# Mixture-of-experts stage of a hybrid layer: GpSimd's arithmetic goes to VectorE, and each tile's weights are written in 16 transfers

## The chip, the cores and the metric

The kernel runs on one core of one Trainium2 chip. The metric is the time of one execution on the device, in microseconds (us). The core has a matrix engine (TensorE, PE in the profile), three engines for elementwise work (VectorE or DVE, ScalarE or ACT, GpSimd or POOL), SyncE (SP), which here only issues transfers, and 16 DMA engines that carry the transfers of all queues.

## The reference

One layer over 512 latent and 256 context tokens of width 1024: a scan (mLSTM) and grouped-query attention side by side, a norm, and then a PEER stage, a product-key mixture of 16384 experts with one hidden unit each. The change lies in the PEER stage and in the norm behind it:

```python
def block(xt):                                   # 128 tokens
    q = (xt @ wq).reshape(P_BLOCK, P_HEADS, 2, P_HALF)
    s = jnp.einsum('nhpd,hpkd->nhpk', q, keys)
    s1, i1 = lax.top_k(s[:, :, 0], P_TOPK)       # 16 of 128 keys, twice for each of 8 heads
    s2, i2 = lax.top_k(s[:, :, 1], P_TOPK)
    cand_s = (s1[..., :, None] + s2[..., None, :])...
    cand_i = (i1[..., :, None] * N_KEYS + i2[..., None, :])...
    top_s, pos = lax.top_k(cand_s, P_TOPK)       # 16 of the 256 pairs
    idx = jnp.take_along_axis(cand_i, pos, axis=-1).reshape(P_BLOCK, P_HEADS * P_TOPK)
    g = jax.nn.softmax(top_s)...
    act = jax.nn.gelu(jnp.einsum('nd,ned->ne', xt, u[idx]), approximate=False)
    return jnp.einsum('ne,ned->nd', g * act, v[idx])
...
x = _layer_norm(DEEPNORM_ALPHA * x + g2 * y, ln2_g[l], ln2_b[l])
```

## The kernel before

Up to about 430 us run the modulation, the projection, the scan, the attention, the output projection and the first norm. The change does not touch them.

From 430 to 570 us comes the head of the PEER stage. `scores` multiplies the tokens with the query weights (line 838) and the queries with the keys (line 846), for two tiles of 128 tokens at a time. `select(t)` finds the top 16 on VectorE. Its part `weigh` turns the position of each chosen pair into two key indices: the position is split into its two ranks (lines 933 to 942), and each rank picks its index by a one-hot comparison with 0 to 15 (line 952, VectorE, f32), a multiply with the 16 indices (line 954, GpSimd) and a reduction over 16 (line 962, VectorE). A cast on GpSimd (line 930) makes the indices f32 first. `prelude(t)` then builds, from one-hot matrices A and B and matmuls (lines 1008 to 1023), the dense table of weights, 128 tokens by 16384 experts, in the tile `work`: 64 KB of each partition. Four transfers of 2 MB on SP's queue write it to the tensor `Wd[t]` in memory (line 1028), each partition's share of a transfer being one run of 16 KB. Then `tables` and `look_up` list the experts that any token of the tile chose.

From 617 to 1253 us run the blocks: four tiles of 29 blocks with 128 experts each. For each block GpSimd issues gathers (line 1108): 128 expert rows of 8 KB (`uv`, 1 MB) and the block's weights from `Wd[t]` (`wr`, 64 KB). A dense block (17 of a tile) transposes the expert rows (line 1268), multiplies them with the tokens (line 1282), applies Gelu on ScalarE (line 1283) and multiplies with the weights on VectorE (line 1284, tile `wt`). A gathered block (12 of a tile) holds experts that one token alone chose: VectorE finds the token (line 1147), GpSimd gathers its row from `h2d` (`xg`, 0.5 MB), VectorE takes the products (line 1168). Both end in two matmuls that add to the tile's result (line 1196, `py`).

Two step lists set the order around the change. In the head, `HEADS` says behind which steps of `select(0)` and `prelude(0)` a query step of tiles 2 and 3 is put. During the blocks of tile t, the generator `ahead` runs `select(t+1)` and `prelude(t+1)`; each step of it has a cost in the list `cost`, and behind each block as many steps are issued as keep the spent cost in line with the blocks done. A scheduler then fixes each engine's order from dependences and priorities. An engine works its instructions in that order, and so does each queue.

When a tile is through, `finish` does the second norm in steps between the next tile's blocks (lines 1248 to 1259): the residual is loaded on GpSimd's queue, the scale and the offset on ScalarE's; VectorE makes the sum (line 1251) and normalises (line 745), GpSimd multiplies with the scale (line 1255) and adds the offset (line 1258).

## Time and profile before

| | |
|---|---|
| median of three runs | 1260.15 us (1259.62 to 1260.58) |
| profiled execution | 1269.07 us |
| its span in the profile | 1267.3 us |
| TensorE (PE) busy | 1051.4 us, 83% |
| VectorE (DVE) busy | 850.2 us, 67% |
| ScalarE (ACT) busy | 467.2 us, 37% |
| GpSimd (POOL) busy | 523.0 us, 41% |
| DMA | 284.16 MB, mean 224 GB/s |
| last chain, by engine | PE 45%, DVE 13%, DMA 9%, issue 5% |

The durations below come from the one profiled execution; a sum made of them is set against its own 1269.07 us. The span runs from the first to the last instruction. The last chain follows the work that ended last back to its start and shares the span out among what it went through. An engine that is busy while another one holds the path costs nothing, and one that waits on the path costs time however little it does. Names such as `work` and `uv` are those of tiles; "xg<-h2d,ti" is an operation that writes `xg` and reads `h2d` and `ti`.

### The profile page before, as it was taken

The page shows a single profiled execution, that of the slowest core. Times are in us where ns is not written, and L with a number is a line of the kernel's source. Part 1 is how long each engine was busy: PE and PEld are TensorE (multiplying, and loading weights), DVE is VectorE, ACT ScalarE, POOL GpSimd, SP SyncE. Part 2 cuts the span into 40 slices and gives each one's busy share as a digit, 9 for nine tenths or more (in the row PEclk, how much of TensorE's full clock was granted, in tenths as well). Part 3 has the DMA queues.
Part 4 walks back from the last instruction along what each step waited for, and adds up shares of the span by engine and source line. Part 5 has one row for each costly group of instructions (what it writes and reads, how often), then busy time and mean ns, then how long its engine had stood idle before and what let it go on. Part 6 is the DMA issues. An engine that isn't in the chain of part 4 may idle for free.

```text
span 1267.3 us, 19149 instructions
## 1 busy us (share of the span) xinstructions
PE 1051.4 (83%) x6784; PEld 844.8 (67%) x6784; DVE 850.2 (67%) x2655; ACT 467.2 (37%) x1132; POOL 523.0 (41%) x404
## 2 busy tenths in 40 slices
PE   6899779699999999993678848769878599597885
PEld 5788679598888888993457725558546477364653
DVE  5958989588857776757748728978479686223123
ACT  4342343555550122444315424234443244432221
POOL 4642423321053411003475513666444755355660
PEclk7899889699999999996789978879988799798988
DMA  9656431310046796228666795488996588988893
GB/s 364 222 200 227 140 134 35 116 41 3 1 151 216 226 264 191 60 91 344 247 255 248 253 364 187 153 293 307 345 410 227 216 291 323 414 314 302 326 350 120
DMA packets 102127, 284.16 MB, mean 224 GB/s; under 512 B 8548, under 2 KB 61512, under 8 KB 83976
## 3 DMA queue, kind: packets, MB, share of 16 engines
q0 software_dynamic: 28480, 158.62, 34.2%
q1 hardware_dynamic: 67656, 115.59, 26.0%
q10 hardware_dynamic: 5888, 8.65, 2.0%
q8 instruction: 55, 0.90, 0.3%
q14 instruction: 48, 0.39, 0.1%
HBM read 237.17 MB, written 45.66 MB: 223 GB/s over the span
## 4 chain that ended last, share of the span: by engine, by line
PE 45%; DVE 13%; DMA 9%; issue 5%; ACT 2%; POOL 2%; another core or an unknown queue 1%; DVEq 0%; ACTq 0%; POOLq 0%
PE py L1196 11%; PE pwq L838 8%; PE s L1282 6%; PE pW L1021 5%; DMA xg<-h2d,ti 5%; PE put L1268 2%; PE pf L1018 2%; DMA wr<-Wd,wi 2%; PE pw L769 2%; PE po L541 2%; DVE work L900 1%; PE ppt L567 1%; DVE work L897 1%; DVE work L898 1%; PE psc L846 1%
## 5 line engine op out<-in xcount | busy, mean ns | idle before, releaser
L1196 PE MATMUL py<-uv,wt 128*128 128x512 f32 x464 | 247.5, 654 | 25.1 <-DVE wt L1284 10.8
L1108 POOL DMA_INDIRECT uv<-in_uv,ri x116 | 120.8, 1041 | 131.9 <-PE py L1196 72.9
L1282 PEld LDWEIGHTS s<-ht,ut 128*128 128x128 f32 x1088 | 143.3, 205 | 40.6 <-ACT wt L1283 21.5
L1282 PE MATMUL s<-ht,ut 128*128 128x128 f32 x1088 | 152.5, 292 | 18.9 <-ACT wt L1283 17.9
L1108 POOL DMA_INDIRECT wr<-Wd,wi x116 | 121.2, 1045 | 54.8 <-issue 29.1
L1196 PEld LDWEIGHTS py<-uv,wt 128*128 128x128 f32 x464 | 84.4, 206 | 83.2 <-issue 54.8
L1269 ACT COPY ut<-put 128x512 f32<-128x512 f32 x136 | 75.3, 588 | 132.1 <-PE put L1268 85.1
L1021 PEld LDWEIGHTS <-A 128*128 128x128 f16 x1024 | 92.7, 147 | 23.1 <-issue 17.4
L1023 ACT ACTIVATE work<-pW 128x512 f32<-128x512 f32 x128 | 74.3, 597 | 89.7 <-PE pW L1021 64.8
L1021 PE MATMUL pW<-B,A 128*128 128x128 f16 x1024 | 98.0, 229 | 9.7 <-ACT work L1023 5.9
L1108 POOL DMA_INDIRECT xg<-h2d,ti x48 | 58.9, 1228 | 96.7 <-DVE ti L1148 44.9
L1268 PE MATMUL put<-cst,uv 128*128 128x128 f32 x544 | 79.4, 286 | 23.2 <-DMA uv<-in_uv,ri 14.4
L1268 PEld LDWEIGHTS put<-cst,uv 128*128 128x128 f32 x544 | 65.8, 149 | 47.3 <-issue 29.4
L838 PE MATMUL pwq<-h2T,wq 128*128 128x256 f32 x416 | 95.0, 380 | 0.0
L1168 DVE SCALAR_TENSOR_TENSOR xg<-xg,uv 128x1024 f32<-128x1024 f32 x48 | 58.6, 1220 | 49.7 <-DMA xg<-h2d,ti 49.7
L1018 PE MATMUL pf<-B,A 128*128 128x128 f16 x512 | 81.3, 230 | 10.5 <-DVE B L1011 10.5
L1011 DVE TENSOR_TENSOR B<-B,igr 128x1024 f16<-128x1024 f16 x128 | 83.3, 687 | 1.2
L838 PEld LDWEIGHTS pwq<-h2T,wq 128*128 128x128 f32 x416 | 76.8, 190 | 9.4 <-DMA wq<-in_wq 0.2
L1018 PEld LDWEIGHTS <-A 128*128 128x128 f16 x512 | 64.2, 148 | 22.2 <-issue 14.5
L1008 DVE TENSOR_TENSOR A<-iob,ig 128x1024 f16<-128x1024 f16 x64 | 46.5, 727 | 48.3 <-PE pW L1021 28.0
L208 POOL TENSOR_TENSOR wlo<-wi,whi 128x1024 fp32r<-128x1024 f32 (+1 forms) x18 | 48.5, 2711 | 59.9 <-ACT whi L207 59.8
L1284 DVE TENSOR_TENSOR wt<-wt,wr 128x128 f32<-128x128 f32 x68 | 25.7, 378 | 63.4 <-ACT wt L1283 52.9
(437 smaller groups left out, 2382.5 us busy)
## 6 DMA issues: line engine op xcount, KB each, us to landing
Wd<-work SPq DMA_DIRECT2D x16, 2048.0 KB, 22.1
wm<-in_w_modT SPq DMA_DIRECT2D x16, 1024.0 KB, 5.0
wq<-in_wq SPq DMA_DIRECT2D x26, 512.0 KB, 4.9
wi<-in_w_in SPq DMA_DIRECT2D x8, 1024.0 KB, 5.5
wsc<-in_w_mod SPq DMA_DIRECT2D x7, 1024.0 KB, 15.6
wor<-in_w_out SPq DMA_DIRECT2D x8, 512.0 KB, 4.2
wql<-in_wq SPq DMA_DIRECT2D x6, 512.0 KB, 5.6
qkT<-in_w_in SPq DMA_DIRECT2D x2, 1024.0 KB
```

Of the source, the lines that this page charges most:

```text
L208: nc.gpsimd.tensor_tensor(lo[:, k:k + 4, 0:cw], wv[:, k:k + 4], hi[:, k:k + 4, 0:cw].bitcast(F32), op=ALU.subtract)
L838: nc.tensor.matmul(pt, w[:, k, :], h2T[:, k, t0 * P:(t0 + 2) * P], start=k == 0, stop=k == KC - 1)
L1011: nc.vector.tensor_tensor(B[:, q].rearrange("p a n r -> p a (n r)"), (B[:, 0] if q else ior).rearrange("p a n r -> p a (n r)"), igr[:, q, ...
L1018: nc.tensor.matmul(pf[:, 0:P], A[:, :, n], B[:, 0, :, n, :], start=c == 0 and n == 0, stop=c == P // TCH - 1 and n == TCH - 1)
L1021: nc.tensor.matmul(pw[:, (n - n4) * P:(n - n4 + 1) * P], A[:, :, n], B[:, q, :, n, :], start=q == 1, stop=q == 2)
L1023: nc.scalar.mul(Wn[:, :, n0 + n4:n0 + n4 + 4], pw.rearrange("p (n k) -> p k n", n=4), 1.0 / GSC)
L1108: nc.gpsimd.indirect_dma_start(out=dst, out_offset=None, in_=src, in_offset=bass.IndirectOffsetOnAxis(ap=ids, axis=0))
L1168: nc.vector.scalar_tensor_tensor(xg, xg, 1.0, w[:, 0:D], op0=ALU.mult, op1=ALU.mult, accum_out=nf)
L1196: nc.tensor.matmul(py[:, hs], wt, w[:, D + half * 512:D + half * 512 + 512], start=i == 0, stop=i == n - 1)
L1268: nc.tensor.transpose(pt[:, q * P:(q + 1) * P], w[:, (4 * kh + q) * P:(4 * kh + q + 1) * P], ident)
L1269: nc.scalar.copy(ut[:, 4 * kh:4 * kh + 4, :], pt.rearrange("p (q n) -> p q n", q=4))
L1282: nc.tensor.matmul(s_[:, 0:P], ut[:, k, :], ht[:, k, :], start=k == 0, stop=k == KC - 1)
```

## The change

GpSimd loses all its arithmetic in the PEER stage. The cast of the indices goes to VectorE and makes f16 (`sih`). The one-hot comparison is made in f16 for all eight heads of a half at once (2048 elements of each partition; 1024 in tile 0, which works on four heads at a time) against a constant `place`, with the sixteen positions in the last dimension but one; the multiply is on VectorE, and four halving adds take the place of the reduction. The norm's two GpSimd instructions become two VectorE instructions that include the normalisation, so that line 745 is no longer called there; its three loads all go to SP's queue, and two more `yield`s stand between its steps. The table of weights goes out in 16 transfers of 512 KB (4 KB of each partition) in place of four; the function `send` issues one behind each later step of `ahead`, and what is left when the first block of the tile comes; in tile 0 all go at once. The costs and `HEADS` change with it.

```diff
-C_SEL, C_OH, C_IIG, C_A, C_L, C_N = 5, 1.5, 6, 3.5, 1.5, 1
+C_SEL, C_OH, C_IIG, C_A, C_L, C_N = 5, 3, 2, 3.5, 1.5, 1
+WPC = 16
...
-HEADS = tuple(range(3, 35, 2))
+HEADS = (2, 4, 6, 8, 10, 12, 14, 16, 18, 21, 24, 27, 30, 33, 38, 40)
...
-            nc.gpsimd.tensor_copy(sif[:, hs].rearrange("p h q a -> p (h q) a"), si[:, 2 * h0:2 * (h0 + gh)])
+            nc.vector.tensor_copy(sih[:, hs].rearrange("p h q a -> p (h q) a"), si[:, 2 * h0:2 * (h0 + gh)])
...
-            n4 = min(gh, 4)
             for q in range(2):
-                for g0 in range(0, gh, n4):
...
-                    nc.vector.tensor_tensor(oh, abf[:, q, g0:g0 + n4].unsqueeze(3).to_broadcast([P, n4, 16, 16]),
-                                            iof[:, 0:16].unsqueeze(1).unsqueeze(1).to_broadcast([P, n4, 16, 16]), op=ALU.is_equal)
-                    eng.tensor_tensor(oh, oh, sif[:, h0 + g0:h0 + g0 + n4, q].unsqueeze(2).to_broadcast([P, n4, 16, 16]), op=ALU.mult)
-                    yield
...
+                nc.vector.tensor_tensor(oh, abh[:, q, 0:gh].unsqueeze(2).to_broadcast([P, gh, 16, 16]),
+                                        place.unsqueeze(1).to_broadcast([P, gh, 16, 16]), op=ALU.is_equal)
+                nc.vector.tensor_tensor(oh, oh, sih[:, hs, q].unsqueeze(3).to_broadcast([P, gh, 16, 16]), op=ALU.mult)
+                yield
+                for w in (8, 4, 2):
+                    nc.vector.tensor_tensor(oh[:, :, 0:w], oh[:, :, 0:w], oh[:, :, w:2 * w], op=ALU.add)
+                nc.vector.tensor_tensor(iig[:, q, ms].rearrange("p (h a) -> p h a", h=gh), oh[:, :, 0], oh[:, :, 1], op=ALU.add)
+                yield
...
-            for q in range(2):
-                oh = scr[:, 4096 * q if t else 4096 + 1024 * q:][:, 0:256 * gh].rearrange("p (m b) -> p m b", b=16)
-                nc.vector.tensor_reduce(iig[:, q, ms], oh, axis=AX.X, op=ALU.add)
...
+    def send(n):
+
+        for _ in range(min(n, len(pieces))):
+            f, q = pieces.pop(0)
+            f(q)
...
-        for q in range(4):
-            ks = slice(q * P // 4, (q + 1) * P // 4)
+        def rows_out(q):
+            ks = slice(q * P // WPC, (q + 1) * P // WPC)
             nc.sync.dma_start(Wd[t][0:NEXP, :].rearrange("(a k) n -> a k n", a=P)[:, ks], Wn[:, ks])
+
+        pieces.extend((rows_out, q) for q in range(WPC))
+        if t == 0:
+            send(WPC)
...
             if i == 0:
+                send(WPC)
                 hts[t] = channels(t, bp if t % 2 else eb)
...
-        nc.gpsimd.dma_start(xt, x1d[ts_, :])
+        nc.sync.dma_start(xt, x1d[ts_, :])
         nc.vector.tensor_tensor(y, y, g2b, op=ALU.mult)
         yield
+        yield
         nc.vector.scalar_tensor_tensor(xt, xt, ALPHA, y, op0=ALU.mult, op1=ALU.add)
-        nc.scalar.dma_start(y, ln2_g.to_broadcast([P, D]))
-        layer_norm(pool, xt, f"l2_{t}")
-        yield
-        nc.gpsimd.tensor_tensor(xt, xt, y, op=ALU.mult)
-        nc.scalar.dma_start(y, ln2_b.to_broadcast([P, D]))
-        yield
-        nc.gpsimd.tensor_tensor(xt, xt, y, op=ALU.add)
+        nc.sync.dma_start(y, ln2_g.to_broadcast([P, D]))
+        mean, r = moments(pool, xt, f"l2_{t}")
+        yield
+        yield
+        nc.vector.scalar_tensor_tensor(xt, xt, mean, y, op0=ALU.subtract, op1=ALU.mult)
+        nc.sync.dma_start(y, ln2_b.to_broadcast([P, D]))
+        yield
+        yield
+        nc.vector.scalar_tensor_tensor(xt, xt, r, y, op0=ALU.mult, op1=ALU.add)
...
+                    send(1)
                     spent += cost[done % len(cost)]
```

What stands on the engines before and now is shown at three places. The first is GpSimd in tile 0's blocks while tile 1 is selected: `uv`, `wr` and `xg` are the gathers of a block, `work` is the selection's tile. Before:

```order
L1108 DMA wr_19_6003<-Wd_3557,wi_5596 128x128
L930 CAST work<-work 128x256
L1108 DMA uv_5_6034<-in_uv,ri_5597 128x2048
L1108 DMA wr_5_6036<-Wd_3557,wi_5596 128x128
L1108 DMA xg_4_6038<-h2d,ti_4_6007 128x1024
L954 TENSOR_TENSOR work<-work 128x1024 x4
L1108 DMA uv_20_6070<-in_uv,ri_5597 128x2048
L1108 DMA wr_20_6072<-Wd_3557,wi_5596 128x128
L1108 DMA uv_6_6148<-in_uv,ri_5597 128x2048
```

The changed kernel at the same place (its lines stand 14 further on):

```order
L1122 DMA wr_19_6029<-Wd_3557,wi_5622 128x128
L1122 DMA uv_5_6060<-in_uv,ri_5623 128x2048
L1122 DMA wr_5_6062<-Wd_3557,wi_5622 128x128
L1122 DMA xg_4_6064<-h2d,ti_4_6033 128x1024
L1122 DMA uv_20_6096<-in_uv,ri_5623 128x2048
L1122 DMA wr_20_6098<-Wd_3557,wi_5622 128x128
```

The cast and the four multiplies are gone, and the gathers follow one another. The second place is VectorE at the same time, from the one-hot comparison of tile 1 (line 952 before, 953 now) on; `jt` and `ti` belong to a gathered block, `wt` is a dense block's multiply. Before:

```order
L952 TENSOR_TENSOR work<-work,iof 128x1024
L942 TENSOR_TENSOR work<-work 128x128
L952 TENSOR_TENSOR work<-work,iof 128x1024
L1284 TENSOR_TENSOR wt_13_5701<-wt_13_5701,wr_13_5621 128x128
L952 TENSOR_TENSOR work<-work,iof 128x1024
L1147 SCALAR_TENSOR_TENSOR jt_1_5720,tk_1_5721<-wr_1_5684,iof 128x128
L952 TENSOR_TENSOR work<-work,iof 128x1024
L1148 TENSOR_SCALAR ti_1_5722<-tk_1_5721 128x1
L1284 TENSOR_TENSOR wt_14_5725<-wt_14_5725,wr_14_5625 128x128
```

Now:

```order
L953 TENSOR_TENSOR work<-work,place 128x2048
L1162 SCALAR_TENSOR_TENSOR jt_1_5746,tk_1_5747<-wr_1_5710,iof 128x128
L943 TENSOR_TENSOR work<-work 128x128
L1163 TENSOR_SCALAR ti_1_5748<-tk_1_5747 128x1
L955 TENSOR_TENSOR work<-work 128x2048
L1303 TENSOR_TENSOR wt_13_5727<-wt_13_5727,wr_13_5647 128x128
L1183 SCALAR_TENSOR_TENSOR xg_0_5712,nf_0_5771<-xg_0_5712,uv_0_5657 128x1024
L1303 TENSOR_TENSOR wt_14_5751<-wt_14_5751,wr_14_5651 128x128
L958 TENSOR_TENSOR work<-work 128x8x128
L953 TENSOR_TENSOR work<-work,place 128x2048
L958 TENSOR_TENSOR work<-work 128x8x64
L955 TENSOR_TENSOR work<-work 128x2048
```

The multiplies (line 955) and the halving adds (line 958) stand between the blocks' instructions, in the place of comparisons alone. The third place is SP's queue from tile 1's weights to the norm of tile 0, with the semaphores that each transfer waits for (DMAHW0 to 7 count transfers that have landed, the others are engines). Before:

```order
L998 DMA igd<-ig_6102 128x512 [waits DVE_49,Activation_49]
L1028 DMA Wd_3558<-work 128x4096 [waits DMAHW4_49,Activation_49,Pool_49]
L1028 DMA Wd_3558<-work 128x4096 [waits DMAHW5_49,Pool_49]
L1028 DMA Wd_3558<-work 128x4096 [waits DMAHW6_49]
L1028 DMA Wd_3558<-work 128x4096
L998 DMA igd<-ig_7629 128x512 [waits DMAHW1_49,DVE_49,Activation_49]
L1259 DMA out<-fx_7464 128x1024 [waits DMAHW3_49,Pool_49]
```

Now, from the first piece on (a row can stand for two pieces):

```order
L1038 DMA Wd_3558<-work 128x1024 [waits DMAHW0_49,Activation_49]
L1038 DMA Wd_3558<-work 128x1024 [waits DMAHW1_49]
L1038 DMA Wd_3558<-work 128x1024 x2
L1038 DMA Wd_3558<-work 128x1024 [waits DMAHW4_49]
L1038 DMA Wd_3558<-work 128x1024
```

and, from the third-last piece on,

```order
L1038 DMA Wd_3558<-work 128x1024 [waits DMAHW5_49]
L1038 DMA Wd_3558<-work 128x1024 [waits DMAHW6_49]
L1038 DMA Wd_3558<-work 128x1024 [waits DMAHW7_49]
L1264 DMA fx_7504<-x1d 128x1024 [waits DMAHW0_49,DVE_49]
L1269 DMA y_7502<-in_ln_g 128x1024 [waits DMAHW1_49,DVE_49]
L1274 DMA y_7502<-in_ln_b 128x1024 [waits DMAHW2_49,DMAHW1_49,DVE_49]
```

Of the 16 pieces only the first waits for an engine; the later ones wait at most for an earlier transfer to land. Behind the last of them come the norm's loads, which before stood on the queues of GpSimd and ScalarE.

## Rows read from the trace of the kernel before

**Rows 1.** Busy time by stage. Columns: the stretch in us and its length; then, for TensorE (PE), its weight load (PEld), VectorE (DVE), ScalarE (ACT) and GpSimd (POOL), busy us and in brackets the instructions; the granted clock of TensorE; the busy share of the 16 DMA engines; GB/s moved. The first line is the head of the PEER stage, the second the blocks.

```profile
430.00:570.00 140.00, 139.77 (x975) 126.53 (x973) 98.49 (x334) 45.19 (x114) 14.46 (x14) 1.00 0.55 161
...
617.00:1253.00 636.00, 512.81 (x3321) 365.30 (x3321) 373.22 (x1208) 224.46 (x595) 338.38 (x294) 0.90 0.78 290
```

**Rows 2.** The chain of work that ended last, in order of time: start in us, length in us, what it was. Two of its steps that are transfers, of token rows out of the tensor `h2d`.

```profile
742.08 13.80 DMA xg<-h2d,ti
...
1074.10 19.59 DMA xg<-h2d,ti
```

**Rows 3.** The same table as in the first group, for five short stretches of the blocks.

```profile
721.00:760.00 39.00, 17.20 (x95) 11.32 (x94) 8.21 (x40) 10.14 (x39) 7.22 (x8) 0.76 0.89 354
760.00:790.00 30.00, 24.38 (x131) 16.20 (x131) 24.95 (x173) 12.89 (x48) 10.46 (x11) 0.85 0.52 187
800.00:832.00 32.00, 19.16 (x79) 11.50 (x77) 31.86 (x52) 9.58 (x17) 22.75 (x13) 0.76 0.44 158
...
965.00:1003.00 38.00, 20.45 (x98) 14.21 (x97) 29.29 (x65) 10.38 (x19) 25.90 (x17) 0.79 0.43 146
1076.00:1110.00 34.00, 18.96 (x102) 11.84 (x101) 8.17 (x44) 15.35 (x65) 11.24 (x13) 0.80 1.00 412
```

**Rows 4.** Timeline of tile 1's selection. Columns here and in the other timelines: start in us, us, engine, line, operation, output<-input, shapes and count, and in square brackets the engine's idle time just before with what ended it.

```profile
652.35 9.26 POOL L954 TENSOR_TENSOR work<-work 128x1024 f32<-128x1024 f32 x4
...
653.72 8.05 DVE L1147 SCALAR_TENSOR_TENSOR jt<-wr,iof 128x128 f32<-128x128 f32 x1 [2.19 <-DMA wr<-Wd,wi]
```

**Rows 5.** Five groups of VectorE instructions, by line. Columns: line, engine, operation, output<-input, count; shortest, median and longest in ns; first and last start in us; the shapes. Line 952 compares 1024 f32 elements of each partition, line 962 reduces 2048 (or, in tile 0, 1024) of them, line 1011 multiplies 1024 f16 elements, line 745 works on a 1024-wide f32 row, line 1147 on 128 elements.

```profile
L952 DVE TENSOR_TENSOR work<-work,iof x16: 1204/1219/4020, 460.6 to 973.8; 128x1024 f32<-128x1024 f32 x16
...
L962 DVE TENSOR_REDUCE iig<-work x10: 1205/2270/2286, 465.3 to 994.5; 128x128 f32<-128x2048 f32 x6, 128x64 f32<-128x1024 f32 x4
...
L1011 DVE TENSOR_TENSOR B<-B,igr x128: 676/685/743, 514.0 to 1060.8; 128x1024 f16<-128x1024 f16 x128
...
L745 DVE TENSOR_SCALAR fx<-fx,lmvl,rrl x3: 811/811/814, 826.6 to 1143.6; 128x1024 f32<-128x1024 f32 x3
...
L1147 DVE SCALAR_TENSOR_TENSOR jt<-wr,iof x48: 232/290/8047, 615.5 to 1237.4; 128x128 f32<-128x128 f32 x48
```

**Rows 6.** Timeline of tile 2's selection, VectorE.

```profile
804.72 2.43 DVE L1284 TENSOR_TENSOR wt<-wt,wr 128x128 f32<-128x128 f32 x1
...
809.74 4.02 DVE L952 TENSOR_TENSOR work<-work,iof 128x1024 f32<-128x1024 f32 x1
...
814.07 3.29 DVE L952 TENSOR_TENSOR work<-work,iof 128x1024 f32<-128x1024 f32 x1
...
818.50 2.28 DVE L101 TENSOR_TENSOR rtl<-rtl,rvl 128x1 f32<-128x1 f32 x1
...
828.03 2.43 DVE L997 TENSOR_TENSOR ig<-gf,ig 128x128 f16<-128x128 f32 x1
```

**Rows 7.** Timeline of tile 3's selection, VectorE.

```profile
974.94 2.43 DVE L1284 TENSOR_TENSOR wt<-wt,wr 128x128 f32<-128x128 f32 x1
...
989.86 2.29 DVE L962 TENSOR_REDUCE iig<-work 128x128 f32<-128x2048 f32 x1 [4.55 <-POOL work L954]
...
994.46 2.29 DVE L962 TENSOR_REDUCE iig<-work 128x128 f32<-128x2048 f32 x1 [2.31 <-POOL work L954]
...
997.93 3.04 DVE L1008 TENSOR_TENSOR A<-iob,ig 128x1024 f16<-128x1024 f16 x1 [1.19 <-ACT ig L994]
```

**Rows 8.** Timeline around the norm of tile 2 (its GpSimd instructions run at 1146 and 1152 us): TensorE's steps with an idle time before them of over 1 us.

```profile
1155.46 1.94 PE L1268 MATMUL put<-cst,uv 128*128 128x128 f32 x8 [3.45 <-DMA uv<-in_uv,ri]
...
1165.39 1.98 PE L1196 MATMUL py<-uv,wt 128*128 128x512 f32 x4 [1.65 <-DVE wt L1284]
...
1170.61 2.08 PE L1196 MATMUL py<-uv,wt 128*128 128x512 f32 x3 [2.32 <-DVE ti L1148]
```

**Rows 9.** DMA queues from 727 to 732 us, while tile 1's weights are written. Columns: queue (q0 is GpSimd's, with the gathers; q1 is that of the other engines' transfers), packets, MB, share of the 16 engines' time. On q0 are token rows of 4 KB, on q1 the weights' rows of 16 KB.

```profile
q1 hardware_dynamic: 110, 1.54, 74.3%
q0 software_dynamic: 107, 0.44, 21.6%
```

**Rows 10.** The same from 599 to 602 us: on q0 gathers of expert rows (8 KB), on q1 loads with rows of 4 KB.

```profile
q0 software_dynamic: 106, 0.59, 49.6%
q1 hardware_dynamic: 117, 0.46, 47.4%
```

**Rows 11.** DMA issues of the page, the writes of the weights: count, KB each, median us from issue to landing.

```profile
Wd<-work SPq DMA_DIRECT2D x16, 2048.0 KB, 22.1
```

**Rows 12.** Timelines of the three stretches in which tables are built: TensorE's steps behind the longest idle times.

```profile
737.66 0.87 PE L1075 MATMUL ppk<-Fw 128*128 128x130 f16 x6 [11.82 <-DVE Fw L1072]
...
757.40 0.29 PE L1054 MATMUL ppr<-trinb,Fw 128*128 128x128 f16 x1 [9.98 <-DVE Fw L1051]
...
918.91 0.29 PE L1053 MATMUL ppr<-trinb,Fw 128*128 128x128 f16 x1 [5.16 <-DVE Fw L1050]
...
925.53 0.29 PE L1054 MATMUL ppr<-trinb,Fw 128*128 128x128 f16 x1 [4.84 <-DVE Fw L1051]
...
1095.15 0.29 PE L1053 MATMUL ppr<-trinb,Fw 128*128 128x128 f16 x1 [13.42 <-DVE Fw L1050]
```

**Rows 13.** Timeline of the head: one query step's 16 matmuls.

```profile
556.20 3.67 PE L838 MATMUL pwq<-h2T,wql 128*128 128x256 f32 x16
```

**Rows 14.** The norm's first GpSimd instruction (line 1255): for what its engine sat idle before it, us in all and times.

```profile
  DMA y<-in_ln_g: 13.0, 2
```

More of the change, by code (lines that the diff above doesn't have):

```diff
@@ L880, in tile_block @@
     pcol = sel.tile([P, 1], F32, name="pcol")
+    place = sel.tile([P, 16, 16], F16, name="place")
     identb = sel.tile([P, P], F16, name="identb")
@@ L912, in select @@
         si = scr[:, 7552:7808].bitcast(U32).rearrange("p (h a) -> p h a", a=16)
-        sif = scr[:, 7808:8064].rearrange("p (h q a) -> p h q a", q=2, a=16)
+        sih = scr[:, 7808:7936].bitcast(F16).rearrange("p (h q a) -> p h q a", q=2, a=16)
         ts = scr[:, 8064:8192].rearrange("p (h a) -> p h a", a=16)
         ti = scr[:, 8192:8320].bitcast(U32).rearrange("p (h a) -> p h a", a=16)
-        abf = scr[:, 8320:8576].rearrange("p (q h a) -> p q h a", q=2, a=16)
+        abh = scr[:, 8320:8448].bitcast(F16).rearrange("p (q h a) -> p q h a", q=2, a=16)
         te = scr[:, 8576:8704].rearrange("p (h a) -> p h a", a=16)
@@ L922, in select @@
         gh = 8 if t else GH
-        eng = nc.gpsimd
         def weigh(h0):
@@ L938, in weigh @@
             nc.vector.tensor_copy(uf[:, 4, 0:m], tif)
-            ab2 = abf.rearrange("p q h a -> p q (h a)")
+            ab2 = abh.rearrange("p q h a -> p q (h a)")
             nc.vector.scalar_tensor_tensor(ab2[:, 0, 0:m], uf[:, 1, 0:m], -12.0, uf[:, 0, 0:m], op0=ALU.add, op1=ALU.max)
@@ L946, in weigh @@
             nc.scalar.activation(te[:, hs], te[:, hs], AF.Exp)
-            n4 = min(gh, 4)
             for q in range(2):
-                for g0 in range(0, gh, n4):
-                    oh = scr[:, (4096 * q if t else 4096 + 1024 * q) + 256 * g0:][:, 0:256 * n4].rearrange(
-                        "p (h a b) -> p h a b", h=n4, a=16)
-                    nc.vector.tensor_tensor(oh, abf[:, q, g0:g0 + n4].unsqueeze(3).to_broadcast([P, n4, 16, 16]),
-                                            iof[:, 0:16].unsqueeze(1).unsqueeze(1).to_broadcast([P, n4, 16, 16]), op=ALU.is_equal)
-                    eng.tensor_tensor(oh, oh, sif[:, h0 + g0:h0 + g0 + n4, q].unsqueeze(2).to_broadcast([P, n4, 16, 16]), op=ALU.mult)
-                    yield
+                oh = scr[:, 4096 + 1024 * q:4096 + 1024 * q + 128 * gh].bitcast(F16).rearrange(
+                    "p (h b a) -> p h b a", h=gh, b=16)
+                nc.vector.tensor_tensor(oh, abh[:, q, 0:gh].unsqueeze(2).to_broadcast([P, gh, 16, 16]),
[6 more added lines that the diff above has]
+                yield
             nc.vector.tensor_reduce(den[:, hs], te[:, hs], axis=AX.X, op=ALU.add)
@@ L979, in select @@
                 yield from weigh(h + 1 - gh)
+    pieces = []
+    def send(n):
+        for _ in range(min(n, len(pieces))):
+            f, q = pieces.pop(0)
+            f(q)
     def prelude(t):
@@ L1292, in tile_block @@
     nc.vector.tensor_copy(ior, iof.rearrange("p (a r) -> p a r", r=RUN).unsqueeze(2).to_broadcast([P, P // RUN, TCH, RUN]))
+    nc.vector.tensor_copy(place, iof[:, 0:16].unsqueeze(2).to_broadcast([P, 16, 16]))
     nc.vector.tensor_copy(identb, ident)
@@ L1324, in tile_block @@
     sy.close()
-    cost = ([C_SEL] * 9 + [C_OH] * 4 + [C_IIG] + [C_A] * (P // TCH) + [C_N] + [C_L] * (NB1[1] // LB) + [C_N]
+    cost = ([C_SEL] * 9 + [C_OH, 1.5] * 2 + [C_IIG] + [C_A] * (P // TCH) + [C_N] + [C_L] * (NB1[1] // LB) + [C_N]
             + [C_L] * -(-(NBL - NB1[1]) // LB) + [C_N])
```

## Prediction

> **What bounds the kernel now.** I read the stages first [rows 1]. From 430 to 570 us TensorE is busy 139.8 of 140 us: there only its own instructions count. In the blocks (617 to 1253 us) it is busy 513 of 636 us, so 123 us are gaps; VectorE is busy 373, GpSimd 338, and the DMA engines 0.78 of the time, which leaves 140 us of DMA time unused. No engine bounds this stage: it loses time where one holds another. Next I read the chain of waits for steps that are waits and not work [rows 2]: gathers of token rows (`xg`) that take 13.8 and 19.6 us to land. Both lie where a tile's dense weights are being written. Then I read the short stretches [rows 3], which are of two kinds. From 721 to 760 and 1076 to 1110 us DMA is at 0.89 and 1.00 and TensorE busy about half: transfers bind. From 800 to 832 and 965 to 1003 us DMA is at 0.44 and 0.43, TensorE again busy little over half, but VectorE is busy 31.9 of 32 and 29.3 of 38 us: VectorE binds, and its time is not all work. The first kind belongs to the writes of the weights, the second to the one-hot places and the norm, which are the two parts of the change.
>
> **GpSimd's arithmetic.** In tile 1, four GpSimd multiplies fill 9.26 us without a break, and the VectorE instruction beside them (128 elements) takes 8.05 us [rows 4], against a median of 0.29 in its group [rows 5]. Nothing it needs is late; it ends as the multiplies end. So a VectorE instruction can be held as long as GpSimd computes. I count the holding at 7.8 us there. In tile 2 five VectorE instructions last 2.43, 4.02, 3.29, 2.28 and 2.43 us [rows 6]; the two of line 952 should take 1.22, the small ones 0.3 at most: some 11.1 us held. In tile 3 it is 2.43 and 3.04 us, for 0.3 and 0.69, with two plain waits for GpSimd of 4.55 and 2.31 [rows 7]: 11.4 us. Around the norm of tile 2 there is no selection, but TensorE's gaps are 3.45, 1.65 and 2.32 us [rows 8], 7.4 in all, of which I give the norm 6.
>
> What takes its place on VectorE, for one tile of 1 to 3, with the prices of [rows 5]: per half an f16 comparison of 2048 elements, a multiply of 2048, and adds of 1024, 512, 256 and 128. An f16 instruction of 1024 takes 0.685, so the comparison takes at most 1.37; I take 1.3. The multiply is between 1.37 and 2.28 (what line 962 takes for 2048 f32 elements, its longer form); I take 2.28, since one of its operands repeats along the innermost dimension, which no f16 instruction of 2048 in the trace does. The adds come to about 0.69 + 0.42 + 0.29 + 0.29 = 1.7. Two halves: 10.5 us, or 8.7 with the cheap multiply. The cast (0.3) and the norm (two of 1024 f32 elements, like line 952's 1.22, less the 0.81 of line 745) bring it to 12.4. Removed are four of 1.22 and two of 2.28, which is 9.4. So VectorE gets 2.9 us more work per tile. What is won where VectorE binds is then 7.8 - 2.9 = 4.9, 11.1 - 2.9 = 8.2 and 11.4 - 2.9 = 8.5, with the norm 6: 28 us. Bounds: nothing (VectorE's held time ran beside TensorE's work, and other waits take over), and 37.6, if the new work fits into holes entirely (7.8 + 11.1 + 11.4 + 7.4).
>
> The Trainium skill, "VectorE: DVE Perf Modes", "What auto-detection actually checks", says that the double rate on two-operand instructions needs every tensor to be 16-bit with a step of one. The 0.685 us of line 1011 (16-bit, step one) against 1.22 for the same count in line 952 (f32) agrees, and by the rule the multiply, with its repeated operand, gets no double rate: 2.28 us, as taken. Were the rule not so, six multiplies would be 0.9 us cheaper each, 5.5 us in all.
>
> **The writes in pieces.** In the order of SP (shown with the change) only the first of the 16 waits for ScalarE; the others wait at most for an earlier transfer to land. So they are not paced by the blocks when they run: they leave one behind another, many at once. What changes for the chip is the row, 4 KB in place of 16 KB. From 727 to 732 us, with token rows of 4 KB against weight rows of 16 KB, the queues moved 107 and 110 packets, almost one for one, so that GpSimd's queue got 0.44 MB and 21.6% of the engines' time [rows 9]. Where SP's queue had rows of 4 KB (599 to 602 us), 106 against 117, GpSimd's queue got 49.6% [rows 10]. So I expect a gather beside the writes to have half the engines, not a fifth: an `xg` of 14 to 20 us in a burst should land in 6 to 9. The writes last longer in return: 2 MB land in 22 us now [rows 11] while taking most of the engines; at half of the 412 GB/s of a full stretch [rows 3] 8.4 MB need about 41 us.
>
> What TensorE lost behind these waits is 11.82 + 9.98 in tile 1, 5.16 + 4.84 in tile 2 and 13.42 in tile 3, 45.2 us [rows 12]. Not all of it can be won: in a stretch where the engines are already full the same bytes have to move, and giving the gathers a larger share only puts the writes off. The win is limited by DMA time that is idle close by. After tile 1's burst that is 0.48 of 30 us, 14.4 us, and 4.3 inside it [rows 3]; behind the bursts of tiles 2 and 3 there is little, since the next tile's gathers wait for the last piece. I take 11 at tile 1 and 1 at each of the others, 13 us. Bounds: nothing, and 45.2.
>
> Against that, rows of 4 KB may use the engines less well: 47.4% of 16 engines for 3 us is 49.4 us of engine per MB [rows 10], 74.3% for 5 us and 1.54 MB is 38.6 [rows 9]. Over 8.4 MB and 16 engines that is 5.7 us a tile, 17 over three. Most of the packet times differ because two queues share the engines, so I take 1 us a tile, 3. Twelve more issues of SP delay nothing: the engine has no computing. Tile 0's pieces pass while tables are built, where the gathers wait in both kernels: nothing, within the 3 us.
>
> **The head.** The one-hot work of tile 0 sits in a stretch where TensorE is full, so cheaper or dearer VectorE work is hidden there; if that cover went, at most a few us. The changed step list puts one more query step ahead of the transpose of tile 0's picks and leaves two at the end where there was one; between them there are fewer. One is 3.67 us of matmuls [rows 13]. A step more at the end costs that, steps that fill former waits give it back: I take -3, from -5 to +3.
>
> **Sum**, against the profiled execution of 1269.07 us: -3 - 28 - 13 + 3 = -41, so 1228. The median of the three runs is 8.9 us below that execution; less the same amount, 1219.
>
> **Rivals.** *The pieces bring nothing* (20%). The Trainium skill, "DMA: Bandwidth & Descriptors", "Queues, rings and completion order", says an engine drains a whole packet of several descriptors from one queue before it turns to another; were a turn worth many rows whatever their length, as that suggests, shorter rows would alter the shares little. The counts of [rows 9, 10], one row for one with both lengths, lean the other way. As a mechanism of this kernel: the gathers keep a fifth of the engines beside the writes, `xg` still takes 14 to 20 us in a burst, and 1269 - 3 - 28 + 3 = 1241, 1232 as a median. The same comes out if the engines are simply full.
>
> *All the burst gaps go* (7%): the gathers get their half, and the writes move entirely into idle time. The 140 us of unused DMA time in the blocks [rows 1] speak for it; the gathers of the next tile, which wait for the last piece, against. 1269 - 3 - 28 - 45 + 3 = 1196, or 1187.
>
> *Taken back by transfers* (6%): a block that computes sooner meets its gather sooner; if the transfers decide at the next full stretch, the 28 us come back as waits there and a time of 1256 to 1262 remains. Against it: DMA at 0.44 and 0.43 just where the gain is made.
>
> *Slower* (9%). The norm's three loads (the residual, the scale, the offset) now gate instructions on VectorE, where the multiply behind each Gelu, which TensorE waits for, stands behind them. On GpSimd the two waits for the scale were 13.0 us in all [rows 14], 6.5 each. Nine such loads are 59 us, and the two `yield`s hide about two blocks (636 / 116 = 5.5 us each) in front of each. It becomes slower than before when more of the 59 us lies bare than the rest wins, 41 us, or 28 if the pieces win nothing; the loads stand on SP's queue, and pieces still going out ahead of them would do it. With 45 bare and nothing from the pieces: 1269 - 3 - 28 + 3 + 45 = 1286, or 1277. Most of these norms run well after the burst, which is against it.
>
> **How the numbers follow.** My forecast has 58%, its own range 1206 to 1234. The range that should hold 8 in 10 reaches up past the first rival into the third and down to the second: 1192 to 1257. A measurement of this kernel tells 0.2%, 2.5 us, from no change. Faster: 58 + 20 + 7 = 85%. Same: 6, the third rival. Slower: 9.
>
> **What would show it.** In the changed kernel's trace no VectorE instruction of 128 elements lasts over 1 us in the blocks, and GpSimd has no arithmetic there; the comparison takes 1.2 to 1.4 us, the multiply 2.3. `xg` in a burst lands in 6 to 9 us, with the queues' shares near half, and each tile's writes take some 40 us. TensorE's gaps of 10 to 13 us behind `Fw` shrink at tile 1 and partly remain at 2 and 3. I am wrong on the first part if VectorE is as full as before at 800 to 832 us with new waits for loads; on the second if `xg` still takes 14 us and more.

## The result and the profile after

The changed kernel takes 1203.13 us (four runs, 1199.05 to 1208.05) against 1260.37 for the kernel before: the ratio is 0.9546, 95% interval 0.9507 to 0.9585, so it is 57 us faster. The prediction was 1219, with 1192 to 1257 as its range; the forecast's own range was 1206 to 1234, and the result lies 3 us below it.

Stage by stage, between the same landmarks in both kernels (430 us, the first write of tile 0's weights, the first write of tile 1's, the copy of tile 0's result, the first writes of tile 2's and tile 3's, the end). Columns as in [rows 1]. Before:

```profile
430.00:564.00 134.00, 133.77 (x942) 121.55 (x941) 96.80 (x323) 44.18 (x111) 14.46 (x14) 1.00 0.54 152
564.00:722.00 158.00, 116.00 (x811) 87.48 (x810) 115.04 (x412) 59.24 (x158) 79.15 (x68) 0.85 0.73 271
722.00:798.00 76.00, 48.57 (x262) 32.66 (x260) 40.67 (x268) 24.46 (x90) 19.09 (x21) 0.82 0.72 277
798.00:901.00 103.00, 86.51 (x665) 64.62 (x664) 84.28 (x165) 40.48 (x83) 67.23 (x51) 0.88 0.74 258
901.00:1069.00 168.00, 134.42 (x953) 98.89 (x952) 122.56 (x446) 66.69 (x176) 92.03 (x79) 0.91 0.80 298
1069.00:1267.00 198.00, 151.61 (x775) 101.42 (x774) 55.43 (x190) 54.84 (x166) 93.56 (x89) 0.90 0.81 309
```

After:

```profile
430.00:563.60 133.60, 133.39 (x939) 120.77 (x938) 93.61 (x343) 43.43 (x110) 3.89 (x8) 1.00 0.53 152
563.60:706.30 142.70, 110.85 (x811) 84.50 (x810) 106.68 (x416) 59.78 (x158) 67.62 (x61) 0.87 0.83 299
706.30:766.40 60.10, 48.46 (x257) 33.63 (x256) 41.98 (x275) 24.21 (x90) 21.21 (x24) 0.86 0.96 363
766.40:852.00 85.60, 80.41 (x668) 61.14 (x666) 74.73 (x178) 39.81 (x84) 51.96 (x45) 0.98 0.85 309
852.00:1011.00 159.00, 133.91 (x953) 98.23 (x951) 117.88 (x451) 65.88 (x177) 76.58 (x71) 0.95 0.85 314
1011.00:1203.00 192.00, 152.50 (x779) 102.51 (x777) 54.35 (x189) 53.93 (x164) 87.01 (x86) 0.91 0.83 316
```

The third number is the stage's length: the gains are 0.4, 15.3, 15.9, 17.4, 9.0 and 6.0 us, 64 in all, which is the difference of the two profiled executions (1269.07 and 1204.68). In the fourth a second thing is to be seen: with the same matmuls (811 and 811, 665 and 668 records, in brackets behind it) TensorE is busy 5.2 us less in the second stage and 6.1 less in the fourth, where its granted clock went from 0.85 to 0.87 and from 0.88 to 0.98 (1.00 is its upper level, 2.4 GHz). In the fourth stage of the kernel before, the low clock lies where VectorE is full and TensorE waits:

```profile
811.00:824.00 13.00, 8.93 (x18) 4.21 (x18) 13.00 (x19) 0.86 (x3) 9.91 (x6) 0.61 0.21 63
```

Over that stage the 128x512 matmuls of `py` took 688 ns on average before, and 623 after.

The parts that answer to the rows of before. VectorE's instructions by line, columns as in [rows 5]: the dense blocks' multiply and the token search, which in [rows 4, 6, 7] lasted 2.4 and 8.05 us, and the new comparison and multiply.

```profile
L1303 DVE TENSOR_TENSOR wt<-wt,wr x68: 271/289/359, 611.7 to 1185.9; 128x128 f32<-128x128 f32 x68
...
L1162 DVE SCALAR_TENSOR_TENSOR jt<-wr,iof x48: 273/285/318, 609.6 to 1174.3; 128x128 f32<-128x128 f32 x48
...
L953 DVE TENSOR_TENSOR work<-work,place x10: 684/1208/1219, 459.7 to 930.2; 128x2048 f16<-128x2048 f16 x6, 128x1024 f16<-128x1024 f16 x4
...
L955 DVE TENSOR_TENSOR work<-work x10: 1219/2278/2300, 460.4 to 931.7; 128x2048 f16<-128x2048 f16 x6, 128x1024 f16<-128x1024 f16 x4
```

The longest time (the third of the three in ns) is the reading: of these two small kinds none lasts over 0.36 us, and none of 128 elements or fewer behind 600 us over 0.43. The comparison takes 1.21 us, where 1.3 was taken, and the multiply 2.28, as taken; for the multiply with its repeated operand the rule of the Trainium skill that it weighed ("VectorE: DVE Perf Modes", "What auto-detection actually checks") is borne out.

The queues from 715 to 725 us, in tile 1's burst of writes (columns as in [rows 9]):

```profile
q0 software_dynamic: 423, 2.38, 62.8%
q1 hardware_dynamic: 422, 1.53, 38.3%
```

423 rows against 422: one for one, and since the write's row is now 4 KB, GpSimd's queue has 62.8% of the engines' time (its rows are of 4 and 8 KB) where it had 21.6%. That holds while both queues are full; over the whole burst, 706 to 750 us, the writes' queue moved its 8.39 MB in 2304 rows beside 1319 of GpSimd's, and the shares are 47.7 and 48.8%. In the chain of waits, the token rows beside tile 2's and tile 3's writes land in 6 to 12 us, not 14 to 20 as in [rows 2]:

```profile
851.43 6.72 DMA xg<-h2d,ti
...
865.33 8.49 DMA xg<-h2d,ti
...
1010.60 6.18 DMA xg<-h2d,ti
...
1028.71 11.96 DMA xg<-h2d,ti
```

TensorE's longest idle times in the three bursts, in the timeline (as [rows 12]):

```profile
722.35 0.29 PE L1067 MATMUL ppr<-trinb,Fw 128*128 128x128 f16 x1 [5.02 <-DVE Fw L1064]
...
738.15 0.48 PE L1089 MATMUL ppk<-Fw 128*128 128x130 f16 x3 [3.93 <-ACT Fw L1095]
...
860.42 0.51 PE L1089 MATMUL ppk<-Fw 128*128 128x130 f16 x3 [5.14 <-DVE Fw L1086]
...
875.28 0.18 PE L1071 MATMUL ppo<-cs,triub 128*128 128x1 f16 x1 [3.59 <-DVE cs L1069]
...
1019.11 0.51 PE L1089 MATMUL ppk<-Fw 128*128 128x130 f16 x3 [4.46 <-DVE Fw L1086]
...
1043.76 0.38 PE L1089 MATMUL ppk<-Fw 128*128 128x130 f16 x2 [5.66 <-ACT Fw L1095]
```

They were 45.2 us in five gaps; these six are 27.8. SP sends the last of a tile's 16 pieces 22 to 28 us after the first, and between them it waits four or five times for an earlier piece to land, 13.6, 9.7 and 7.3 us in all for the three tiles. The queue sets their pace, then, and not the blocks.

### The profile page after: what moved, and what is told of

Read it like the earlier page. It is cut to its first block, busy times and chain, and to the rows that moved or that the text cites. A ratio compares the mean times of both kernels' runs of the same rounds, so it can differ in the third digit from the quotient of the medians.

```text
span 1202.9 us, 19211 instructions
## 1 busy us (share of the span) xinstructions
PE 1038.4 (86%) x6784; PEld 837.7 (70%) x6784; DVE 826.4 (69%) x2698; ACT 464.8 (39%) x1132; POOL 465.7 (39%) x374
## 4 chain that ended last, share of the span: by engine, by line
PE 38%; DVE 16%; DMA 10%; issue 8%; ACT 2%; SPq 1%; POOL 1%; another core or an unknown queue 0%; DVEq 0%; ACTq 0%; POOLq 0%
PE py L1211 8%; PE pwq L839 8%; PE s L1301 4%; DMA xg<-h2d,ti 4%; PE pW L1031 3%; PE pw L770 2%; PE put L1287 2%; PE po L542 2%; DMA Wd<-work 2%; DVE work L900 2%; DMA uv<-in_uv,ri 2%; DVE work L899 1%; DVE work L902 1%; DVE work L901 1%; PE pf L1028 1%
## 5 line engine op out<-in xcount | busy, mean ns | idle before, releaser
L1211 PE MATMUL py<-uv,wt 128*128 128x512 f32 x464 | 239.7, 636 | 14.6 <-DVE wt L1303 7.8
L1122 POOL DMA_INDIRECT wr<-Wd,wi x116 | 125.6, 1083 | 69.5 <-issue 35.6
L1031 PEld LDWEIGHTS <-A 128*128 128x128 f16 x1024 | 89.7, 146 | 20.3 <-issue 13.1
L1031 PE MATMUL pW<-B,A 128*128 128x128 f16 x1024 | 95.3, 225 | 6.4 <-ACT work L1033 2.9
L1287 PEld LDWEIGHTS put<-cst,uv 128*128 128x128 f32 x544 | 68.3, 152 | 41.8 <-issue 29.9
L1122 POOL DMA_INDIRECT xg<-h2d,ti x48 | 57.9, 1206 | 94.1 <-DVE ti L1163 44.6
L1183 DVE SCALAR_TENSOR_TENSOR xg<-xg,uv 128x1024 f32<-128x1024 f32 x48 | 58.5, 1219 | 46.5 <-DMA xg<-h2d,ti 46.4
L1018 DVE TENSOR_TENSOR A<-iob,ig 128x1024 f16<-128x1024 f16 x64 | 44.0, 688 | 47.6 <-ACT ig L1004 27.8
L1028 PE MATMUL pf<-B,A 128*128 128x128 f16 x512 | 75.0, 226 | 1.1 <-issue 1.0
L1028 PEld LDWEIGHTS <-A 128*128 128x128 f16 x512 | 60.5, 147 | 8.4 <-issue 6.4
L1303 DVE TENSOR_TENSOR wt<-wt,wr 128x128 f32<-128x128 f32 x68 | 19.6, 289 | 58.1 <-ACT wt L1302 58.1
```

The source lines that it names most:

```text
L1028: nc.tensor.matmul(pf[:, 0:P], A[:, :, n], B[:, 0, :, n, :], start=c == 0 and n == 0, stop=c == P // TCH - 1 and n == TCH - 1)
L1031: nc.tensor.matmul(pw[:, (n - n4) * P:(n - n4 + 1) * P], A[:, :, n], B[:, q, :, n, :], start=q == 1, stop=q == 2)
L1122: nc.gpsimd.indirect_dma_start(out=dst, out_offset=None, in_=src, in_offset=bass.IndirectOffsetOnAxis(ap=ids, axis=0))
L1183: nc.vector.scalar_tensor_tensor(xg, xg, 1.0, w[:, 0:D], op0=ALU.mult, op1=ALU.mult, accum_out=nf)
L1211: nc.tensor.matmul(py[:, hs], wt, w[:, D + half * 512:D + half * 512 + 512], start=i == 0, stop=i == n - 1)
L1287: nc.tensor.transpose(pt[:, q * P:(q + 1) * P], w[:, (4 * kh + q) * P:(4 * kh + q + 1) * P], ident)
```

## The experiments

The experiments ran in three groups on three chips, and the kernel before takes 1232, 1257 and 1260 us on them. So only ratios to the kernel before of the same group are compared, and times only within a group.

**The parts alone, first chip (before: 1232.11 us).** *Only the pieces* is the kernel before with

```diff
+WPC = 16
-        for q in range(4):
-            ks = slice(q * P // 4, (q + 1) * P // 4)
+        def rows_out(q):
+            ks = slice(q * P // WPC, (q + 1) * P // WPC)
...
+                    send(1)
```

> The kernel before with the weights written in 16 pieces and nothing else. If the length of the rows sets how the queues share the DMA engines, the gathers beside the writes land sooner: 12 to 20 us faster, 1240 to 1248, with the TensorE gap behind the first table build of tile 1 (11.8 us before) under 7. If the pieces bring nothing and the whole gain is GpSimd's, 1257 to 1263 with that gap as before.

Measured: 1231.57, ratio 0.9984 (0.9957 to 1.0010). Neither answer came out whole: the time is that of the second, but the gap behind the first table build of tile 1 is 7.58 us (the first answer had it under 7). The trace of the norm alone (below), on the same chip and with four writes, has that gap at 11.80:

```profile
720.73 0.87 PE L1075 MATMUL ppk<-Fw 128*128 128x130 f16 x6 [11.80 <-DVE Fw L1072]
```

So the shares moved as the row theory has it, and yet the time did not. What stands against the gain is seen at the other two boundaries. At tile 3's the chain of waits goes twice through the writes themselves (start, length, what), and then a gather waits for them:

```profile
1046.67 17.88 DMA Wd<-work
1064.56 23.57 DMA Wd<-work
...
1088.94 0.95 POOL L1121 DMA_INDIRECT wr<-Wd,wi  x1 [15.22 <-DMA Wd<-work]
```

41 us behind pieces that began at 1039: SP sends the last piece only when an earlier one has landed, and the next tile's gathers, which need the whole table, came to stand behind it. At tile 2's boundary it is VectorE that waits, since the next selection writes into `work`, out of which the pieces still go:

```profile
902.76 0.49 DVE L897 MAX8 work<-scfx 128x8 f32<-128x128 f32 x2 [13.30 <-DMA Wd<-work]
```

TensorE's longest gap there, 12.05 us, ends with that selection. Since the kernel before has no trace on this chip, that these waits are all of what took the gain is not shown.

*Only the one-hot places* has the f16 `weigh`, its costs and `HEADS`, and keeps four writes and the norm of before:

```diff
-                    eng.tensor_tensor(oh, oh, sif[:, h0 + g0:h0 + g0 + n4, q].unsqueeze(2).to_broadcast([P, n4, 16, 16]), op=ALU.mult)
+                nc.vector.tensor_tensor(oh, oh, sih[:, hs, q].unsqueeze(3).to_broadcast([P, gh, 16, 16]), op=ALU.mult)
```

> The kernel before with the f16 one-hot places on VectorE, their costs and the changed step list of the head, and nothing else. If GpSimd's arithmetic held VectorE in the selection and the new VectorE work fits into holes: 30 to 38 us faster, 1222 to 1230, and no small VectorE instruction over 1 us but where the norm still runs on GpSimd. If the new VectorE work eats most of it, as the recorded sum has it with 2.9 us a tile: 20 to 26 faster, 1234 to 1240.

Measured: 1198.83, ratio 0.9719 (0.9684 to 0.9755), 33 us faster: the first answer. The new VectorE work did not eat the gain. The costs and `HEADS` move the order of instructions too, and no run separates that.

*Only the norm* has the changed lines of `finish` (1248 to 1258) alone:

```diff
-        nc.gpsimd.tensor_tensor(xt, xt, y, op=ALU.mult)
+        nc.vector.scalar_tensor_tensor(xt, xt, mean, y, op0=ALU.subtract, op1=ALU.mult)
```

> The kernel before with the norm on VectorE and its loads on SP's queue, and nothing else. If GpSimd's four instructions in the norm cost what the TensorE gaps beside them showed: 4 to 9 us faster, 1251 to 1256. If the loads that now gate VectorE cost more than they free: 1262 or above.

Measured: 1225.57, ratio 0.9934 (0.9902 to 0.9966), 6.5 us faster by the medians (8 by the ratio), the first answer; what its loads cost VectorE is less than what they free.

*The changed kernel with four writes* differs from it by one number:

```diff
-WPC = 16
+WPC = 4
```

> The changed kernel with 4 writes of 16 KB rows in place of 16 of 4 KB rows. If the row length counts, it loses what the pieces bring: 12 to 20 us, 1215 to 1223, with gathers of token rows of 13 us and more beside the writes. If the pieces bring nothing: 1200 to 1207.

Measured: 1199.33, ratio 0.9707 (0.9670 to 0.9744). On this chip the one-hot part alone does as much as one-hot and norm together, so the gains don't add. The time lies in neither answer: both were written in us for a kernel before of 1260, and the changed kernel did not run on this chip. The next group has it.

**Before, after and four writes on one chip (before: 1257.43 us).** The two unchanged kernels first:

> The kernel before, unchanged, for its trace on the chip of this call: the calls so far showed 1260 and 1232 us for it. If the chips differ in the blocks alone, its head up to 570 us is as long as in the first trace, and the difference lies at the writes of the weights and in the gathers.

> The changed kernel, unchanged, on the same chip. If the pieces are worth nothing on this chip, the ratio to before is that of the one-hot work and the norm together, 0.965 to 0.975; if they are worth what the first comparison left over, 0.95 to 0.96.

Measured: 1259.40 and 1195.72, ratios 1.0008 (0.9979 to 1.0037) and 0.9509 (0.9463 to 0.9555), in the second answer's range. The trace of before is close to the first one, in the two gaps of tile 1 too (11.81 and 10.13 us for 11.82 and 9.98; tile 3's is 11.38 for 13.42). For the first chip's 1232 there is no trace of the kernel before, so what makes it faster there is not shown.

> The changed kernel with 4 writes of 16 KB rows, beside the changed kernel on one chip. If the row length counts, 8 us or more slower than the changed kernel; if the pieces bring nothing, within 3 us of it.

Measured: 1209.57, ratio 0.9615 (0.9571 to 0.9658): 14 us slower than the changed kernel. So in the company of the other parts the pieces are worth 14 us here. Its queues from 715 to 725 us show the shares behind it:

```profile
q1 hardware_dynamic: 214, 3.23, 75.4%
q0 software_dynamic: 212, 1.04, 25.0%
```

214 rows against 212, and 75.4% of the time for the writes. TensorE's two longest gaps in each of the three bursts make 42.2 us here, and 29.9 in the changed kernel on the same chip.

**GpSimd's arithmetic by itself (same chip).** The changed kernel with, in each half of `weigh` for tiles 1 to 3,

```diff
+                if t:
+                    for _ in range(2):
+                        nc.gpsimd.tensor_tensor(scr[:, 0:D], scr[:, 0:D], scr[:, D:2 * D], op=ALU.mult)
```

> The changed kernel with four GpSimd multiplies of 1024 f32 elements in each later tile's selection, on data that nothing reads, as long as those that the change removed. If GpSimd's arithmetic by itself holds VectorE (and the gathers behind it), VectorE instructions of 128 elements again last over 2 us and it loses 10 to 30 us. If the loss came from VectorE's waits for GpSimd's results, there are none here, and it is within 5 us of the changed kernel.

Measured: 1219.49, ratio 0.9687 (0.9639 to 0.9735), 24 us slower than the changed kernel, though no instruction needs the products. The scheduler put tile 1's four ahead of the blocks, at 565 us, where tables are built, and three of tile 2's into the burst of writes; the other five lie in the selections. In the timeline of tile 3's:

```profile
929.54 2.28 DVE L955 TENSOR_TENSOR work<-work 128x2048 f16<-128x2048 f16 x1
930.46 3.56 POOL L958 TENSOR_TENSOR work<-work 128x1024 f32<-128x1024 f32 x1
931.74 2.43 DVE L1306 TENSOR_TENSOR wt<-wt,wr 128x128 f32<-128x128 f32 x1
...
946.77 5.12 DVE L955 TENSOR_TENSOR work<-work 128x2048 f16<-128x2048 f16 x1
...
947.37 2.36 POOL L958 TENSOR_TENSOR work<-work 128x1024 f32<-128x1024 f32 x1
```

The dense blocks' multiply takes 2.43 us again, and a 2.28 us instruction takes 5.12 beside a GpSimd multiply of 2.36: about as long as both together. So GpSimd's arithmetic holds VectorE with no dependence between them. The Trainium skill, "SBUF — State Buffer", "Who interferes with whom", calls this an exclusive lock on a shared pair of ports, where the second to come is blocked until the first instruction ends. The first three rows agree: GpSimd's multiply, behind a VectorE multiply that had begun, takes 3.56 us for 2.36, and then VectorE waits for it. In the last two VectorE's record starts 0.60 us ahead and VectorE is yet the one held, and [rows 4] go beyond the rule (last section).

The 24 us are not all holding. Against the changed kernel on the same chip the stages lose 8.9, 0.9, 3.4, 7.2 and 4.1 us from tile 0's first write on, and the last of them has no GpSimd arithmetic at all. In the first, a load of tile 1's scores stands behind the four multiplies on GpSimd's queue, and VectorE waits for it, which it does not in the changed kernel:

```profile
584.04 0.49 DVE L898 MAX8 work<-scfx 128x8 f32<-128x128 f32 x2 [4.02 <-DMA scfx<-scd]
```

How much of the rest is holding was not measured.

**The multiply back on GpSimd, third chip (before: 1259.99 us).**

```diff
-                nc.vector.tensor_tensor(oh, oh, sih[:, hs, q].unsqueeze(3).to_broadcast([P, gh, 16, 16]), op=ALU.mult)
+                (nc.gpsimd if t else nc.vector).tensor_tensor(oh, oh, sih[:, hs, q].unsqueeze(3).to_broadcast([P, gh, 16, 16]), op=ALU.mult)
```

> The changed kernel with the f16 multiply of the later tiles back on GpSimd, so that VectorE waits for it and the order of the engines is again the later one (the weights' matmuls begin four blocks later in tile 1). Idle multiplies of this length cost 24 us. If holding is all, 20 to 28 us slower than the changed kernel (0.967 to 0.973 of before); if the later order and the waits cost as well, 30 to 40 us slower (0.975 to 0.983).

Measured: 1228.39, ratio 0.9754 (0.9726 to 0.9782): 31 us above the 0.9509 of the changed kernel, in the second answer's range. A GpSimd multiply of 2048 f16 elements takes 3.66 us, so its six are 22 us where the twelve idle ones were 28: less arithmetic, and it costs 7 us more (by ratios, on two chips that run the kernel before alike). Waits for the result are not it: in the blocks of this trace no VectorE instruction waits for GpSimd's `work`. All six lie in the selections, though, where of the idle ones five did, and the order is another; which of the two costs the 7 us was not tried.

**Length of the rows or number of writes (third chip).** Eight writes of 8 KB rows (`WPC = 8`):

> The changed kernel with 8 writes of 8 KB rows. If the row's length sets the share, token rows get about a third of the engines beside the writes and the time lies between those with 4 and with 16 writes, 3 to 10 us above the changed kernel; if it is a gain of splitting as such, as the changed kernel.

Measured: 1204.26, ratio 0.9573 (0.9541 to 0.9605), between those of 4 and 16 writes, 0.9615 and 0.9509, though its interval overlaps both and they come from another chip. The queues from 715 to 725 us stand between as well:

```profile
q1 hardware_dynamic: 339, 2.42, 58.1%
q0 software_dynamic: 336, 1.77, 42.4%
```

339 rows against 336. Then 16 writes of 16 KB rows, each of 32 partitions:

```diff
-            ks = slice(q * P // WPC, (q + 1) * P // WPC)
-            nc.sync.dma_start(Wd[t][0:NEXP, :].rearrange("(a k) n -> a k n", a=P)[:, ks], Wn[:, ks])
+            ks = slice(q // 4 * P // 4, (q // 4 + 1) * P // 4)
+            gs = slice(q % 4 * P // 4, (q % 4 + 1) * P // 4)
+            nc.sync.dma_start(Wd[t][0:NEXP, :].rearrange("(a k) n -> a k n", a=P)[gs, ks], Wn[gs, ks])
```

> The changed kernel with 16 writes per tile whose rows are 16 KB long: each piece takes 32 partitions, not all 128. If the length of a row sets the queues' shares, a gather of token rows beside the writes gets a fifth again, and the time is that of the changed kernel with 4 writes (0.962 of before on the chip where the changed kernel has 0.951). If the number of writes counts, that of the changed kernel.

and 4 writes of 4 KB rows:

```diff
-WPC = 16
+WPC = 4
...
+            nc.sync.dma_start(Wd[t][0:NEXP, :].rearrange("(a j q r) n -> a j q (r n)", a=P, j=4, q=4)[:, :, q],
+                              Wn.rearrange("p (j q r) n -> p j q (r n)", j=4, q=4)[:, :, q])
```

> The changed kernel with 4 writes per tile whose rows are 4 KB long: each takes four runs of 4 KB of every partition. If the row's length counts, packets go about one for one, the gathers get half, and the time is that of the changed kernel (0.951 of before). If the number of writes counts, 0.962.

Measured: 1343.60 (ratio 1.0663, 1.0631 to 1.0696) and 1242.69 (0.9867, 0.9833 to 0.9901). Both times fall outside either answer, and they answer nothing, since in both the next selection comes later. In the first, all of a next tile's top-16 instructions stand in one lump on VectorE, between the last lists and the blocks; that the scheduler, which orders the engines ahead of time, took this shape for a slow transfer is a guess. In the second each of the four writes takes parts from all over `work`, into which the next selection writes, and its first instruction waits until they have landed, 47 us after the first was sent (28 in the changed kernel):

```profile
755.93 0.49 DVE L898 MAX8 work<-scfx 128x8 f32<-128x128 f32 x2 [9.68 <-DMA Wd<-work]
```

The stretches behind the first burst, of the first kernel and of the second (columns as in [rows 1]):

```profile
800.00:850.00 50.00, 7.89 (x37) 6.20 (x36) 46.97 (x214) 5.61 (x9) 9.56 (x11) 0.56 0.24 84
...
750.00:790.00 40.00, 18.98 (x87) 12.43 (x87) 31.06 (x212) 5.06 (x10) 12.86 (x14) 0.70 0.49 181
```

VectorE is busy 47 of 50 us and TensorE 7.9; in the second, 31 and 19 of 40. What can still be read is inside the bursts: the queues of the first from 740 to 750 us, and of the second from 720 to 730.

```profile
q1 hardware_dynamic: 215, 2.38, 74.2%
q0 software_dynamic: 188, 1.17, 27.9%
...
q1 hardware_dynamic: 543, 2.16, 54.3%
q0 software_dynamic: 282, 1.85, 47.3%
```

With 16 writes of long rows the writes have 74% of the time and a token row takes 22.6 us in the chain; with 4 writes of short rows they have 54%. In the second window the gathers' queue is not always full: in its first half the rows are 192 of the gathers against 185 of the writes, and the writes have 35.7%; in its second they are 90 against 358. The shares go with the row's length and not with the number of writes. What the number is worth in time stays open.

## Why the prediction was right, and where it was short

*GpSimd holds VectorE* was right, in its place and its kind: no instruction is held any more, the parts alone give 33 and 6.5 us on one chip, and arithmetic that nothing reads brings the holding back, with a part of the loss. The size was off. The sum took 2.9 us of new VectorE work off each tile, and put 4.9, 8.2 and 8.5 us to the three selections. The idle time of TensorE in the stages that hold them (length less busy time, from the first two tables) fell by 10.2 in the second stage, of which up to 3.8 belong to the head (below) and some to the tables; by 11.3 in the fourth, which is the 11.1 that were counted as held, with nothing taken off; and by 8.5 in the fifth, which is the sum's own figure. So the new VectorE work hid in the fourth stage; for the other two this is not shown.

*The clock* is the term that is missing from the sum. Matmuls of the second and fourth stages took 11.3 us less for the same work, as the granted clock rose. The fifth stage does not fit as well: 0.91 to 0.95, and 0.5 us less. The rows held the granted clock, and the prediction gave it no line. That fewer gaps raise it is an inference from these two stages, where it rose as idle time fell; no run set it by itself, and how much of the 11.3 us it is stays open.

*The writes* came out by rows as forecast: one for one where both queues are full, with 62.8% there and 48.8% over the burst for the gathers, `xg` in 6 to 9 us but for one of 12, and some 44 us for tile 1's writes where 40 were forecast. The turn worth many rows whatever their length, which the first rival weighed, does not show in the shares. Where the gain lies was not as forecast. The tile-1 burst is 15.9 us shorter where 11 were given it, but not by the pieces alone: on the second chip that stretch is 73.7 us before, 64.7 in the changed kernel with four writes and 59.0 with 16, so that 5.7 us of it are theirs. The price of short rows, 1 us a tile, was about right: 38.3% of 16 engines for 10 us is 40 us of engine per MB, and 38.6 was the reading for long rows [rows 9]. The forecast of 10 us net stands against 14 on one chip with the rest, spread over all stages behind the first write, and none on another without it; that the 14 are so near is in part luck. The rival that the pieces bring nothing described that second run, by another way than it said: the share changed, and the later end of the writes stood against the gain. Two things differ between the runs, the chip and the rest of the change, and none of the kernels separates them.

*The norm* was put at 6 us and gave 6.5 alone. The slower rival's price, loads that lie bare on VectorE, was paid in part: in the trace after, VectorE waits once for the scale, 4.4 us, and twice for the offset, 8.1 us, of the 59 us that it reckoned with. (Each of the norm's three steps has two `yield`s ahead of it now, so three more in all, where the section on the change says two.)

*The head* was put at -3; the first matmul of tile 0's tables comes 3.8 us sooner (567.11 and 563.29 us). *The conversion* to the median took 8.9 us off for a span that the profiled execution of before had over its median; after, it is 1.6 us. In profiled times the forecast, 1228, was 23 us above the 1204.68, in medians 16: 7 us of the miss are hidden by that conversion, which is luck.

## What to carry to other kernels

GpSimd arithmetic beside a busy VectorE cost VectorE its own time here, even on data that nobody shares: read an instruction's longest duration against its median, and price the removal by TensorE's gaps and not only by the difference of the two engines' work. Two queues that are both full shared the DMA engines row for row in these runs, so a bulk transfer with long rows starves gathers with short ones; shorter rows give the gathers their share but delay the end of the bulk transfer, so look first at what waits for that end, be it a reader of the table or the next writer of the buffer. Before an experiment on the shape of a transfer, look at the instruction order that the scheduler makes of it and at when its source buffer comes free, since these can move more than the transfer.

## What was not expected of the hardware

How long VectorE is held differs between runs of the same instructions. In [rows 4] it waited from 653.72 us to the end of four multiplies. With the norm alone changed, on the first chip, the same four are as long, and VectorE gets in between them:

```profile
640.69 9.56 POOL L954 TENSOR_TENSOR work<-work 128x1024 f32<-128x1024 f32 x4
...
645.31 0.38 DVE L1147 SCALAR_TENSOR_TENSOR jt<-wr,iof 128x128 f32<-128x128 f32 x1 [4.29 <-DMA wr<-Wd,wi]
...
646.37 1.67 DVE L1288 TENSOR_TENSOR wt<-wt,wr 128x128 f32<-128x128 f32 x1 [0.68 <-ACT wt L1287]
```

A multiply is 2.4 us, so one ends at 645.5 and one at 647.9; the instruction that came at 645.31 ran at once, the one that came at 646.37 ended at 648.0. In the other kernel VectorE let three such ends pass. It is not the chip: in the kernel with the pieces alone, on the same first chip, VectorE is held again past two ends (GpSimd's multiplies end at 647.28 and 649.57 us) to that of the fourth.

```profile
642.61 9.25 POOL L955 TENSOR_TENSOR work<-work 128x1024 f32<-128x1024 f32 x4
...
646.27 5.75 DVE L1161 SCALAR_TENSOR_TENSOR jt<-wr,iof 128x128 f32<-128x128 f32 x1 [4.49 <-DMA wr<-Wd,wi]
```

What decides it is not shown.
